# Ends of ada sums moved into the first FFN's last units, and mixer casts ordered behind the mLSTM decays, in a one-layer kernel on one core

## The chip, the cores and the metric

The kernel runs on one core of a Trainium2 chip. The metric is the device time of one execution in microseconds (us); of several runs the median counts. A core has five engines that each take their own queue of instructions in order: TensorE (PE, matrix products), VectorE (DVE), ScalarE (ACT), GpSimd (POOL) and SyncE (SP). SP only issues DMAs here; an issue that waits for a free buffer holds up all that is behind it in SP's queue. Products land in PSUM banks, all else lies in SBUF.

## What is computed

One transformer layer on 256 tokens of width 2048, all in float32: a SwiGLU FFN, a token mixer and a second SwiGLU FFN, each with a modulated layer norm ahead of it and a gated residual with a layer norm behind it. The mixer has eight softmax heads with forget gates ("fox") and four mLSTM heads.

```python
ada = (jax.nn.silu(c) @ w_ada + b_ada)[:, None, :]
sh1, sc1, g1, sh2, sc2, g2, sh3, sc3, g3 = jnp.split(ada, N_ADA, axis=-1)
h = _swiglu(_modulate(x, sh1, sc1), ffn1_w_in, ffn1_w_out)
x = _layernorm(ALPHA * x + 0.5 * (1 + g1) * h, ln1_g, ln1_b)
h = _token_mixer(_modulate(x, sh2, sc2), w_in, ..., w_out)
x = _layernorm(ALPHA * x + (1 + g2) * h, ln2_g, ln2_b)
h = _swiglu(_modulate(x, sh3, sc3), ffn2_w_in, ffn2_w_out)
x = _layernorm(ALPHA * x + 0.5 * (1 + g3) * h, ln3_g, ln3_b)
```

An mLSTM head weighs products of queries and keys with a matrix of decays, exp(-relu(running maximum - key's gate)) under a causal mask, multiplies that by its values and divides by a row's sum.

## The kernel before

**Products.** A float32 product is made of three products of split parts: each operand is cast to a shorter type (`hi`, ACT, `split`, L149) and what the cast leaves is subtracted out (`lo`, DVE); `mm3` (L398) adds hi*hi, hi*lo and lo*hi. Weights are loaded 1 MB at a time by `load_w` (L370): one DMA on SP into one of three `raw` buffers, then casts and subtractions in halves of 1024 columns into six `hi` and six `lo` buffers. Such a load is called a unit here. In the mixer, `form_a_four` (L1111) makes four feature tiles from four units of 48 matmuls each: its calls for the mLSTM queries and keys are named m0 and m1, those for the fox heads 4 to 7 fb (queries) and fbk (keys), for heads 0 to 3 fa and fak. So fbk0 is the first unit of fbk. `cols_form_b` (L1075) does the same with tokens in the rows; its loads already stand behind an instruction (`emptied`).

**The ada sums.** The nine modulation vectors need all of `w_ada`, 16 rows of 512 KB for each of 18 pieces, and go on beside everything else. An `AdaQueue` (L214) holds the pieces in order (2_0, 2_1, 3_0 to 3_3, 6_0, then others that wait for a later `stage`). `pump(n)` (L252) is called once a unit: it adds n to `owed`, moves the oldest finished piece one step through its end (`tail`), then traces as many rows as are owed. A row is a DMA into one of two `ar` buffers and a multiply-add on DVE (`ada_acc`, L161). The end of a piece like 3_3 (`pair_tail`, L188) has five steps: cast and subtract its first half (`ahi`, `alo`); nothing; sum it over partitions with two matmuls (`bc`, L178), pick the diagonal (`dg`, L195), reduce it (L197) and split the second half; nothing; the same sum for the second half and an addition (L199). `ahi`, `alo` and `dg` have one buffer each, `dg` the one of `alo`. `need(n)` (L263) runs whatever is missing until n pieces are done, and sets `owed` to 0 where anything was missing. `pump` traces under `pinned`, which puts DVE's part behind the latest subtractions of the main work; `need` doesn't.

**The first FFN's output.** `out_proj` (L431) goes over column groups of 1024, 512 and 512. In the last group (`lastg`) of 11 units the last four only load, cast and subtract; their products are kept (`held`) and are issued in `finish1` (L977), at the boundary to the mixer, where the layer norm follows. `npump` is called for the first seven units of that group. The fourth and fifth steps of 3_3's end are left to `need(6)` in `finish1`.

**The mixer.** Beside the weight products run side jobs, Python generators in a list; after each unit `step` (L1062) pumps the ada queue and advances up to three of them (`advance`, L1048). A head's first step (`mlstm_head`, L1293) makes the gate matrix `gb` (L1301), the scores `sps` (L1303; the larger one in the only buffer of tag `m5`, the smaller in the rest of `gb`'s bank), and from them on ACT a Relu (L1306) and an exponential (L1307) for each of two blocks, and on DVE the mask (L1308) and the product with the scores (L1309), called the masks below. Its second step multiplies by the values (`nps`, L1315) and normalizes (L1320 to L1325). Head 1's step can follow head 0's by one unit.

**Order.** Each instruction is traced in program order and then placed by the framework's scheduler, which gives an engine the earliest-traced instruction that it takes to be ready. So an instruction that was traced later can stand ahead in the queue; the chip then keeps the queue's order. `tc.issue_after(i)` places what a block traces on i's engine behind i on that engine's queue. In blocks under `tc.manual_schedule` (the boundaries' DVE and ACT work) the traced order is kept.

Of the kernel before, what the change touches and what calls it, by code (L numbers as in the profile page):

```python
# [32 lines left out]
def layer_kernel(  # L33
# [107 lines left out]
    @contextmanager  # L141
    def pinned():
        with ExitStack() as s:
            for i in pin.values():
                s.enter_context(tc.issue_after(i))
            yield
# [67 lines left out]
    class AdaQueue:  # L214
# [19 lines left out]
        def row(self):  # L234
# [14 lines left out]
                self.rows = None  # L249
            return True  # L250

        def pump(self, n):  # L252
            self.owed += n
            with pinned():
                if self.tails:
                    self.tail()
            while self.owed >= 1:
                with pinned():
                    if not self.row():
                        break  # L260
                self.owed -= 1

        def need(self, n):  # L263
            while self.done < n:
                self.owed = 0
                if self.tails:
                    self.tail()
                else:
                    self.row()
# [161 lines left out]
    def out_proj(w, rows, nk, tag, npump, finish, before=None, turned=False, spare=None, fine=None):  # L431
        st = [stat_tile(f"{tag}{a}") if a == 0 or fine is None else fine for a in range(2)]
        nheld = 4 if spare else 3
        col = 0
        late = []


        def catch_up(n):
            while n and late:
                if next(late[0], 0) == 0:  # L440
                    late.pop(0)
                else:
                    n -= 1
        for width in (1024, 512, 512):
            nb, kn = width // 512, 2048 // width
            nu = nk // kn
            us = list(range(nu))
            if turned:
                us = us[nu // 2:] + us[nu // 4:nu // 2] + us[:nu // 4]
            ps = {(a, b): mm_tile(f"o_{tag}{col}{a}{b}") for b in range(nb) for a in range(2)}  # L450
            lastg = col + width == D
            held = []

            def products(a, args, last=us[-1] * kn + kn - 1):
                ts_ = slice(a * P, (a + 1) * P)
                for k, hh, hl, hi, lo in args:
                    for b in range(nb):
                        mm3(ps[a, b], hh[:, ts_], hl[:, ts_], hi[:, b * 512:(b + 1) * 512],
                            lo[:, b * 512:(b + 1) * 512], k == us[0] * kn, k == last)

            def half_products(outs):
                for c, o in enumerate(outs):
                    cs = slice(c * 256, (c + 1) * 256)
                    for n, (k, hh, hl, hi, lo) in enumerate(held):
                        mm3(o[:, :256], hh[:, P:], hl[:, P:], hi[:, cs], lo[:, cs], n == 0, n == len(held) - 1)

            def add_stats(cs):
                if fine is None:
                    V.bn_stats(st[1][:, cs.start // 512, :], res[:, 1, cs])
                else:  # L470
                    for i in range(cs.start // 256, cs.stop // 256):
                        V.bn_stats(st[1][:, i, :], res[:, 1, i * 256:(i + 1) * 256])

            def add_halves(outs, col=col):
                for c, o in enumerate(outs):
                    cs = slice(col + c * 256, col + (c + 1) * 256)
                    r = res[:, 1, cs]
                    V.tensor_tensor(out=o[:, :256], in0=o[:, :256], in1=gate[:, cs], op=ALU.mult)
                    yield
                    V.tensor_tensor(out=r, in0=r, in1=o[:, :256], op=ALU.add)  # L480
                    yield
                    add_stats(cs)
                    yield

            def add_up(a, ps=ps, col=col, bs=range(nb), stats=True):
                for b in bs:
                    cs = slice(col + b * 512, col + (b + 1) * 512)
                    r = res[:, a, cs]
                    V.tensor_tensor(out=ps[a, b], in0=ps[a, b], in1=gate[:, cs], op=ALU.mult)
                    yield  # L490
                    V.scalar_tensor_tensor(out=r, in0=r, scalar=ALPHA, in1=ps[a, b],
                                           op0=ALU.mult, op1=ALU.add)
                    yield
                    if a and stats:
                        add_stats(cs)
                    elif stats:
                        V.bn_stats(st[0][:, col // 512 + b, :], r)
                    yield

            for i, u in enumerate(us):  # L500
                hs = []
                if before:
                    before(u * kn)
                into = spare() if spare and lastg and i == nu - nheld else None
                for k in range(u * kn, u * kn + kn, 2):
                    hs += rows(k)
                for kk, hi, lo in load_w(w[u * kn * P:(u + 1) * kn * P, col:col + width], kn, width,
                                         f"{tag}o{col}_{u}", into=into):
                    arg = (u * kn + kk, *hs[kk], hi, lo)
                    if lastg and i >= nu - nheld or not lastg and i == nu - 1:  # L510
                        held.append(arg)
                    else:
                        for a in range(2):
                            if a and lastg and fine is not None:
                                products(a, [arg], nk - nheld * kn - 1)
                            else:
                                products(a, [arg])
                if not lastg and i == nu - 1:

                    late += [add_up(a, bs=(b,)) for b in range(nb) for a in range(2)]  # L520
                    products(0, held)
                    catch_up(2)
                    products(1, held)
                else:
                    catch_up(2)
                if not lastg or i < nu - 4:
                    npump()
            if lastg:
                catch_up(99)
                if fine is None:  # L530
                    finish(lambda a: products(a, held), add_up, st)
                else:
                    for _ in add_up(1, stats=False):
                        pass
                    outs = [mm_tile(f"o_{tag}last{c}") for c in range(2)]
                    finish(lambda a: half_products(outs) if a else products(0, held),
                           lambda a: add_halves(outs) if a else add_up(0), st)
            else:
                col += width
# [436 lines left out]

    def finish1(products, add_up, st):  # L977
        need(6)
        products(0)
        products(1)  # L980
        ent["dead"].release()
        hp.release()
        ent["xp"] = tc.alloc_tile_pool(name="xp2", bufs=1)
        gap(ent["xp"], 544, "gap_x")
        ent["np"] = tc.alloc_tile_pool(name="np2", bufs=1)
        ent["f"] = (add_up, st)
# [83 lines left out]


    emptied = [None]


    def cols_form_b(c0, col, ws, use, name, four=False):  # L1075
# [35 lines left out]
    def form_a_four(c0, name, before_last=lambda: None):  # L1111
        ps = [mm_tile(f"pr_{name}{i}", True) for i in range(2)]
        for u in range(4):
            if u == 3:
                before_last()
            for k4, hi, lo in load_w(W[u * 512:(u + 1) * 512, c0:c0 + 512], 4, 512, f"{name}{u}"):
                k = 4 * u + k4
                for f in range(4):
                    fs = slice(f * P, (f + 1) * P)
                    mm3(ps[f // 2][:, f % 2 * T:(f % 2 + 1) * T], hi[:, fs], lo[:, fs], xhi[:, k, :], xlo[:, k, :],  # L1120
                        k + f % 2 == 0, k + f % 2 == KD)
            step()
        return [ps[f // 2][:, f % 2 * T:(f % 2 + 1) * T] for f in range(4)]

# [168 lines left out]
    def mlstm_head(o, h):  # L1293
# [10 lines left out]
        for i in range(2):  # L1304
            d = dm[:, i * T:T + i * P]
            S.activation(d, gb[:, i * P:T], AF.Relu, bias=nacol[:, i, h:h + 1])  # L1306
            S.activation(d, d, AF.Exp, scale=-1.0)  # L1307
            V.tensor_tensor(out=d[:, :P], in0=d[:, :P], in1=triu1[:, :P], op=ALU.mult)  # L1308
            V.tensor_tensor(out=d, in0=sps[i], in1=d, op=ALU.mult)  # L1309
        done.add(f"o{h}")  # L1310
# [282 lines left out]
```

## Time and profile before

| | us |
|---|---|
| median of 3 runs | 1928.33 |
| lowest, highest | 1928.22, 1933.65 |
| the profiled execution | 1927.28 |
| its span, first to last instruction | 1925.6 |

The rows of the profile read as follows. A row of the timeline is: start, length in us, engine, line, operation, what is written from what, shape, count (merged neighbours), and in brackets the engine's idle time before it and what ended that. A row of the waits is: engine and what it was to run, then what it waited for, us in total, times, longest. A row of the windows is: stretch, its length, an engine's busy time (and instructions), granted TensorE clock (1.00 is full speed), busy share of the DMA engines, GB/s. Tile names have their numbers left out: `lo_fbk` stands for all eight halves of the units fbk0 to fbk3. In the list of DMA issues stand the count, the size and the median time in us from issue to landing.

### The profile page before, as it was taken

What the parts mean: (1) busy time and instruction counts of PE and PEld (TensorE: products, weight loads), DVE (VectorE), ACT (ScalarE), POOL (GpSimd) and SP (SyncE); (2) the same over time, 40 slices, a digit from 0 to 9 for tenths busy, and PEclk for the clock granted to TensorE, in tenths of its full rate; (3) what the DMA queues carried; (4) which work ended last, traced back from release to release, by engine and by line L of the source; (5) the groups of instructions that cost most, each with busy time, mean ns of one, the idle gap of its engine ahead of it and who ended that gap; (6) DMA issues with size and microseconds to landing.
All of it is one profiled execution on the core that took longest, in us unless ns stands there. A gap on an engine that the chain in (4) does not pass through costs nothing.

```text
span 1925.6 us, 32413 instructions
## 1 busy us (share of the span) xinstructions
PE 1891.5 (98%) x13133; PEld 1724.6 (90%) x13133; DVE 1483.4 (77%) x1847; ACT 953.7 (50%) x1359; POOL 59.7 (3%) x88
## 2 busy tenths in 40 slices
PE   6999999999999999999999999999999999999997
PEld 3999999999988887699989886999999999988886
DVE  6788989877789898888988887867766655555776
ACT  3554454444454555845655645565444444444562
POOL 1111100000000000100000000000000000000000
PEclk9999999999999999999999999999999999999999
DMA  9978969999898787499988883987777766755552
GB/s 359 375 262 313 328 218 296 337 331 306 266 339 296 267 301 236 138 321 317 319 300 272 315 300 114 338 282 246 262 248 260 246 213 196 240 184 189 196 196 89
DMA packets 283662, 510.92 MB, mean 265 GB/s; under 512 B 10962, under 2 KB 134514, under 8 KB 282488
## 3 DMA queue, kind: packets, MB, share of 16 engines
q1 hardware_dynamic: 275640, 480.53, 73.4%
q0 software_dynamic: 7872, 28.32, 4.4%
q8 instruction: 103, 1.69, 0.4%
q14 instruction: 47, 0.39, 0.1%
HBM read 506.71 MB, written 2.10 MB: 264 GB/s over the span
## 4 chain that ended last, share of the span: by engine, by line
PE 84%; DVE 7%; DMA 5%; issue 2%; ACT 1%; SPq 0%; DVEq 0%; POOL 0%; ACTq 0%
PE gu_f L401 8%; PE gu_f L400 8%; PE gu_f L399 8%; PE o_f L399 6%; PE o_f L401 6%; PE o_f L400 6%; PE s L400 4%; PE s L399 4%; PE s L401 4%; DMA ar<-in_w_ada_dram 3%; PE fs L401 1%; PE fs L399 1%; PE fs L400 1%; PE o_mx L399 1%; PE o_mx L401 1%
## 5 line engine op out<-in xcount | busy, mean ns | idle before, releaser
L165 DVE SCALAR_TENSOR_TENSOR acc<-ar,csil,acc 128x1024 f32<-128x1024 f32 (+1 forms) x167 | 211.4, 1267 | 52.2 <-DMA ar<-in_w_ada_dram 51.5
L400 PE MATMUL s<-xlo_f,hi_s 128*128 128x256 f32 x768 | 213.6, 278 | 1.2 <-DVE xlo_f L331 1.2
L399 PE MATMUL s<-xhi_f,hi_s 128*128 128x256 f32 x768 | 213.4, 279 | 0.0
L401 PE MATMUL s<-xhi_f,lo_s 128*128 128x256 f32 x768 | 213.3, 278 | 0.0
L401 PE MATMUL gu_f<-xhi_f,lo_f2i 128*128 128x256 f32 x768 | 212.0, 276 | 0.0
L399 PE MATMUL gu_f<-xhi_f,hi_f2i 128*128 128x256 f32 x768 | 212.0, 276 | 0.0
L400 PE MATMUL gu_f<-xlo_f,hi_f2i 128*128 128x256 f32 x768 | 212.0, 276 | 0.0
L151 DVE TENSOR_TENSOR lo_f2i<-raw_f2i,hi_f2i 128x1024 fp32r<-128x1024 f32 x96 | 117.4, 1224 | 92.4 <-ACT hi_f2i L150 92.4
L401 PE MATMUL gu_f<-xhi_f,lo_f1i 128*128 128x256 f32 x640 | 176.7, 276 | 0.0
L399 PE MATMUL gu_f<-xhi_f,hi_f1i 128*128 128x256 f32 x640 | 176.7, 276 | 0.0
L400 PE MATMUL gu_f<-xlo_f,hi_f1i 128*128 128x256 f32 x640 | 176.7, 276 | 0.0
L150 ACT CAST hi_f2i<-raw_f2i 128x1024 fp32r<-128x1024 f32 x96 | 100.8, 1050 | 135.4 <-PE gu_f L400 124.6
L150 ACT CAST hi_s<-raw_s 128x1024 fp32r<-128x1024 f32 x96 | 100.6, 1052 | 130.3 <-PE s L400 93.4
L400 PEld LDWEIGHTS s<-xlo_f,hi_s 128*128 128x128 f32 x768 | 145.5, 189 | 1.5 <-DVE xlo_f L331 1.5
L401 PEld LDWEIGHTS s<-xhi_f,lo_s 128*128 128x128 f32 x768 | 145.4, 189 | 0.0
L399 PEld LDWEIGHTS s<-xhi_f,hi_s 128*128 128x128 f32 x768 | 144.9, 189 | 0.0
L399 PEld LDWEIGHTS gu_f<-xhi_f,hi_f2i 128*128 128x128 f32 x768 | 144.2, 188 | 0.2
L400 PEld LDWEIGHTS gu_f<-xlo_f,hi_f2i 128*128 128x128 f32 x768 | 144.2, 188 | 0.2
L401 PEld LDWEIGHTS gu_f<-xhi_f,lo_f2i 128*128 128x128 f32 x768 | 144.2, 188 | 0.0
L151 DVE TENSOR_TENSOR lo_f2o<-raw_f2o,hi_f2o 128x1024 fp32r<-128x1024 f32 x86 | 105.2, 1223 | 43.3 <-ACT hi_f2o L150 43.3
L165 DVE SCALAR_TENSOR_TENSOR gate<-ar,csil,gate 128x1024 f32<-128x1024 f32 (+1 forms) x94 | 117.5, 1251 | 25.4 <-DMA ar<-in_w_ada_dram 25.2
L151 DVE TENSOR_TENSOR lo_s<-raw_s,hi_s 128x1024 fp32r<-128x1024 f32 x96 | 115.5, 1219 | 27.4 <-ACT hi_s L150 27.2
(478 smaller groups left out, 5511.6 us busy)
## 6 DMA issues: line engine op xcount, KB each, us to landing
ar<-in_w_ada_dram SPq DMA_DIRECT2D x227, 512.0 KB, 5.4
raw_f2i<-in_ffn_w_in_dram SPq DMA_DIRECT2D x48, 1024.0 KB, 5.2
raw_s<-in_ffn_w_in_dram SPq DMA_DIRECT2D x47, 1024.0 KB, 7.6
raw_f1o<-in_ffn_w_out_dram SPq DMA_DIRECT2D x44, 1024.0 KB, 7.3
raw_f2o<-in_ffn_w_out_dram SPq DMA_DIRECT2D x44, 1024.0 KB, 5.1
raw_f1i<-in_ffn_w_in_dram SPq DMA_DIRECT2D x40, 1024.0 KB, 7.4
ar<-in_w_ada_dram POOLq DMA_DIRECT2D x48, 512.0 KB, 6.9
raw_mxo<-in_w_out_dram SPq DMA_DIRECT2D x16, 1024.0 KB, 6.0
```

The lines of the kernel that those rows point to most:

```text
L150: S.copy(hi, src)
L151: return V.tensor_tensor(out=lo, in0=src, in1=hi.bitcast(F32), op=ALU.subtract)
L165: V.scalar_tensor_tensor(out=acc, in0=raw, scalar=csil[:, k:k + 1], in1=acc, op0=ALU.mult, op1=ALU.add)
L399: PE.matmul(o, ah, bh, start=start, stop=False)
L400: PE.matmul(o, ah, bl, start=False, stop=False)
L401: PE.matmul(o, al, bh, start=False, stop=stop)
```

## The change

In the first FFN's output, the last four units of the last group, which don't pump, now each move the oldest finished ada piece one step through its end, if there is one; no rows are traced there. `finish1` sets `owed` to 0 behind `need(6)`. In the mixer, each unit of `form_a_four` takes the last exponential that an mLSTM head traced, two units back, and places its casts behind it on ACT: `decays[1]` is written by a head's step, `decays[0]` is read by the units, and a unit moves one into the other behind its products and ahead of its own step.

```diff
+        def end_step(self):
+            if self.tails:
+                with pinned():
+                    self.tail()
+
         def pump(self, n):
             self.owed += n
-            with pinned():
-                if self.tails:
-                    self.tail()
+            self.end_step()
             while self.owed >= 1:
...
                 if not lastg or i < nu - 4:
                     npump()
+                elif tag == "f1":
+                    ada.end_step()
...
     def finish1(products, add_up, st):
         need(6)
+        ada.owed = 0
         products(0)
...
     emptied = [None]
+    decays = [None, None]
...
-            for k4, hi, lo in load_w(W[u * 512:(u + 1) * 512, c0:c0 + 512], 4, 512, f"{name}{u}"):
+            for k4, hi, lo in load_w(W[u * 512:(u + 1) * 512, c0:c0 + 512], 4, 512, f"{name}{u}",
+                                     behind=decays[0]):
                 k = 4 * u + k4
...
+            decays[:] = decays[1], None
             step()
...
             S.activation(d, gb[:, i * P:T], AF.Relu, bias=nacol[:, i, h:h + 1])
-            S.activation(d, d, AF.Exp, scale=-1.0)
+            decays[1] = S.activation(d, d, AF.Exp, scale=-1.0).ins
```

## The prediction

> **What bounds the kernel now.** I read the totals first, then who TensorE waits for, then the stretch around the longest wait on TensorE, ScalarE (ACT) and VectorE (DVE).
>
> ```profile
> span 1925.6 us, 32413 instructions
> PE 1891.5 (98%) x13133; PEld 1724.6 (90%) x13133; DVE 1483.4 (77%) x1847; ACT 953.7 (50%) x1359; POOL 59.7 (3%) x88
> ```
>
> TensorE is idle for 34 us of 1925.6, so every gain must come out of a hole in its queue, or out of time in which it runs slowly. The waits of TensorE from the end of the first FFN to the end of the mixer (us in total, times, longest) are few:
>
> ```profile
> PE sps L1303 <- DVE dm L1309: 4.1, 1, 4.1
> ...
> PE bc L178 <- DVE alo L151: 0.9, 1, 0.9
> PE bc L178 <- ACT ahi L150: 0.5, 1, 0.5
> ```
>
> Both parts of the change stand beside one of them: the ends of the ada sums beside the two `bc` rows, the mixer casts beside the 4.1 us of `sps`. The stretches around the latter, TensorE alone (length, busy, count, granted clock, DMA share, GB/s):
>
> ```profile
> 963.72:964.40 0.68, 0.68 (x6) 1.00 0.94 380
> ...
> 969.98:974.36 4.38, 0.28 (x3) 1.00 0.92 317
> 974.36:975.07 0.71, 0.71 (x4) 0.95 1.00 381
> 975.07:982.22 7.15, 7.15 (x50) 0.77 0.99 354
> 982.22:984.22 2.00, 2.00 (x14) 1.00 1.03 337
> 984.22:989.78 5.56, 5.56 (x51) 1.00 0.87 292
> 989.78:990.89 1.11, 1.11 (x8) 1.00 1.09 345
> ```
>
> The first row is head 0's block (`gb`, `sps`), undisturbed. The second and third are head 1's: 5.09 us instead of 0.68, because its `sps` writes the one `m5` bank that head 0's masks must have been read out of. The fourth is the next unit of 48 weight matmuls, 7.15 us where the same unit takes 5.56 at full clock. So the hole costs (5.09 - 0.68) + (7.15 - 5.56) = **6.00 us**. Why head 0's masks are late, ACT first, then DVE:
>
> ```profile
> 962.14 0.20 ACT L1283 ACTIVATE rq_exp<-o 128x1 f32<-128x1 f32 x1
> 962.38 2.00 ACT L150 CAST hi_fbk<-raw_fbk 128x1024 fp32r<-128x1024 f32 x2
> 966.32 2.00 ACT L150 CAST hi_fbk<-raw_fbk 128x1024 fp32r<-128x1024 f32 x2 [1.94 <-DMA raw_fbk<-in_w_in_dram]
> 968.23 0.72 ACT L1306 ACTIVATE dm<-gb,nacol 128x256 f32<-128x256 f32 x2
> 968.84 0.61 ACT L1307 ACTIVATE dm<-dm 128x256 f32<-128x256 f32 x2
> ```
> ```profile
> 964.51 1.27 DVE L165 SCALAR_TENSOR_TENSOR acc<-ar,csil,acc 128x1024 f32<-128x1024 f32 x1
> 965.71 1.22 DVE L151 TENSOR_TENSOR lo_fbk<-raw_fbk,hi_fbk 128x1024 fp32r<-128x1024 f32 x1
> 967.61 1.28 DVE L165 SCALAR_TENSOR_TENSOR acc<-ar,csil,acc 128x1024 f32<-128x1024 f32 x1 [0.69 <-DMA ar<-in_w_ada_dram]
> 968.81 2.35 DVE L151 TENSOR_TENSOR lo_fbk<-raw_fbk,hi_fbk 128x1024 fp32r<-128x1024 f32 x2
> ...
> 971.68 1.21 DVE L151 TENSOR_TENSOR lo_fbk<-raw_fbk,hi_fbk 128x1024 fp32r<-128x1024 f32 x1
> ...
> 973.41 0.28 DVE L1308 TENSOR_TENSOR dm<-dm,trir 128x128 f32<-128x128 f32 x1
> ...
> 974.23 0.28 DVE L1309 TENSOR_TENSOR dm<-gb,dm 128x128 f32<-128x128 f32 x1
> 974.42 1.27 DVE L165 SCALAR_TENSOR_TENSOR acc<-ar,csil,acc 128x1024 f32<-128x1024 f32 x1
> ```
>
> Head 0's `gb` is written by 964.0 (first stretch), yet the four decay instructions start at 968.23: four casts of units fbk0 and fbk1 are queued ahead of them, and the third waits 1.94 us for its weights. The exponentials end at 969.45; on DVE the masks (973.41 to 974.51) then stand behind the subtractions that those casts released. Nothing is short of work: it is an order.
>
> **The change, part by part.** *Casts behind the decays.* It adds and removes no instruction; it orders ACT alone. A step's last exponential goes into `decays[1]`, the next unit moves it to `decays[0]`, so it binds the unit after that. Counting the side queue's steps, heads 0 to 3 run after units fb2, fb3, fbk0 and fbk2. TensorE's `gb` agrees, at 963.72 and 969.98 by the stretches above and for heads 2 and 3 here:
>
> ```profile
> 983.33 0.47 PE L1301 MATMUL gb<-ng,rowsel 128*128 128x256 f32 x1
> ...
> 997.99 0.38 PE L1301 MATMUL gb<-ng,rowsel 128*128 128x256 f32 x1
> ```
>
> So fbk0's casts go behind head 0, fbk1's behind head 1, fbk2's behind head 2, fa0's behind head 3. I follow that in the clock of before:
>
> Head 0: ACT is free from 962.34, the decays run from 964.05 for 1.22 us (968.23 to 969.45) to 965.3, fbk0's casts to 967.3. On DVE the row of 964.51 ends at 965.8, the masks take 1.1 us to 966.9, the two `lo_fbk` of 1.2 us and the row of 967.61 (1.28) follow until 970.6. TensorE wants `sps` at 969.98 and no longer waits; head 1's block ends at 970.66, where it wants the first half of fbk0 (ready at 968.1) and 2.8 us later the second. The hole's 6.00 us go.
>
> Head 1: `gb` at 969.98, decays until 971.5, casts until 973.5, subtractions until about 976 with one row between. Wanted at 970.66 + 5.56 + 2.00 = 978.2. Hidden.
>
> Head 2 is the tight one:
>
> ```profile
> 986.50 0.84 ACT L1324 ACTIVATE yM<-nps,dn 128x256 f32<-128x256 f32 x2 [1.27 <-DVE dn L1323]
> ...
> 988.02 0.61 ACT L1307 ACTIVATE dm<-dm 128x256 f32<-128x256 f32 x2
> ...
> 1000.30 0.61 ACT L1307 ACTIVATE dm<-dm 128x256 f32<-128x256 f32 x2
> ```
> ```profile
> 984.98 1.21 DVE L151 TENSOR_TENSOR lo_fbk<-raw_fbk,hi_fbk 128x1024 fp32r<-128x1024 f32 x1
> ...
> 988.06 1.28 DVE L165 SCALAR_TENSOR_TENSOR acc<-ar,csil,acc 128x1024 f32<-128x1024 f32 x1 [1.34 <-DMA ar<-in_w_ada_dram]
> ```
>
> Its exponentials stand behind head 0's normalising (L1324), which waits for DVE, and end 5.3 us after `gb` (983.33 to 988.63). In the new clock `gb` is at 976.22 + 1.11 = 977.3, so exponentials to 982.6, first cast (1.05) 983.7, subtraction (1.22) 984.9; TensorE wants fbk2 at 978.22 + 5.56 + 1.11 = 984.9. No slack, if DVE is as busy; but the `lo_fbk` at 984.98, among the reciprocals that L1324 waits for, is a later unit's and now comes afterwards, which gives 1.2 us back. A row with a late load (1.28 + 1.34) instead costs up to 2.6. Head 3: exponentials end 2.9 us after `gb` (997.99 to 1000.91); wanted 6.3 us after it (0.8 block, 5.56 unit), less 2.3 for cast and subtraction: 1.1 to spare. New waits lie between 0 and 3 us; I take 0.4, nearer to 0 as the subtraction does leave the reciprocals' way. The DMAs of later units start when the casts free their `raw` buffers, some 6 us nearer to their use; fa1 would still load at 985 for a use past 1003.
>
> *Ends of the ada sums.* `need(6)` at the boundary ran the last two steps of sum 3_3 (an empty one, then two `bc` matmuls, `dg`, its reduction, an addition); they are now traced behind units 7 and 8. The queue's bookkeeping gives `done` 6 there, `need(6)` falls through, and `owed = 0` repeats what its loop did: from the mixer on, the same rows in the same steps, no DMA moved. TensorE's queue has nothing between the old place and the new, since units 7 to 10 only cast and their products come in `finish1`. What it waits for:
>
> ```profile
> 755.14 0.50 PE L178 MATMUL bc<-ahi,trir 128*128 128x512 f32 x1 [0.48 <-ACT ahi L150]
> 759.55 0.50 PE L178 MATMUL bc<-alo,trir 128*128 128x512 f32 x1 [0.94 <-DVE alo L151]
> ```
> ```profile
> 757.07 0.69 DVE L197 TENSOR_REDUCE scsh<-dg 128x4 f32<-128x512 f32 x1
> 757.67 1.22 DVE L151 TENSOR_TENSOR lo_f1o<-raw_f1o,hi_f1o 128x1024 fp32r<-128x1024 f32 x1
> 758.81 0.68 DVE L151 TENSOR_TENSOR alo<-acc,ahi 128x512 fp32r<-128x512 f32 x1
> ```
>
> `ahi` and `alo` belong to the step before, traced behind unit 6 in both kernels, and `alo` needs the buffer that the reduction at 757.07 frees. The change moves neither. I take 0; the bounds are -1.4 (both waits gone) and +0.5 (the moved reduction, 0.69, ahead of a subtraction).
>
> *Sum.* -6.0 + 0.4 + 0 = -5.6. The profiled execution took 1927.28 us (span 1925.6 and 1.7 around it), giving 1921.7; the median of the runs is 1.05 above it, so 1928.33 - 5.6 = **1922.7**.
>
> [...]
>
> **The rivals.**
> *The masks stay late (the change does not do what it says).* ACT's order is bound, DVE's is not. If the row now at 974.42 takes the place left by the subtractions, the masks wait for its load:
>
> ```profile
> 965.82 3.45 SPq L184 DMA_DIRECT2D ar<-in_w_ada_dram  x2
> ```
> ```profile
> ar<-in_w_ada_dram SPq DMA_DIRECT2D x227, 512.0 KB, 5.4
> ```
>
> Issued at 965.82, with 5.4 us to land: 971.2, row until 972.5, masks until 973.6, `sps` 0.8 us earlier than now: about 1927.5. For it: that row came directly after the masks. Against it: it is later in the program than they are.
>
> *The part ends pay too*: both `bc` waits go, 1922.7 - 1.4 = 1921.3. Against it stands the unmoved `alo`.
>
> *Half of it is given back*: fbk2 waits 2.6 us as worked out for a late row: 1922.7 + 2.6 - 0.4 = 1924.9.
>
> *Slower*: the casts held back starve TensorE. Where the reciprocals of head 0 and of head 2 each stand behind a row whose load was only just issued (5.4 us), fbk2 waits 5.4 - 1.2 = 4.2 and fa0 5.4 - 1.1 = 4.3 us. Both exceed the 4.1 us hole that brought the slow unit, so each adds 1.59: 11.7 - 6.0 = +5.7, 1934.0. It outweighs the gain once the two waits exceed 6 us together. For it: DVE's rows above follow one another without a gap from 968.81 on, so whatever is late there stays late. Against it: rows are queued behind subtractions of their own unit, so a late one needs the order of before to change.
>
> **How the numbers follow.** Forecast 0.48, own range 1921.0 to 1924.5; masks late 0.18; part ends pay 0.10; half given back 0.10; slower 0.14. From 1920.7 to 1930.5 some 0.15 is left out, most of it above. A measurement of this kernel tells 0.3% (5.8 us) from no change; the forecast's 5.6 lies just inside. Faster by more: 0.22 of the forecast's 0.48 and the part ends' 0.10, 0.32. Slower by more: over half of the slow case, 0.08. Within: 0.60.
>
> **What would show it.** Right: the `sps` row gone from TensorE's waits, L1306 at about 964 and ahead of the first `hi_fbk`, the unit after head 1 at 5.6 us and full clock, both `bc` waits still there. Wrong: `dm` L1308 behind three rows of `acc`; `pr_fbk` or `pr_fa` waiting for `lo`; the `bc` waits gone; waits behind the mixer that were not there.

## The result, and the profile after

| kernel | runs | median, us | lowest, highest | ratio to before [95% interval] |
|---|---|---|---|---|
| before | 22 | 1929.36 | 1926.21, 1935.96 | |
| changed | 22 | 1925.14 | 1919.49, 1931.73 | 0.9976 [0.9968, 0.9983] |

The change takes 0.24% off: 4.6 us by the ratio, 4.2 by the two medians. That is in the predicted range of 1920.7 to 1930.5 and near the forecast's -5.6, though above the forecast's own range, which ended at 1924.5. The profile shows that it came about in another way than forecast, and in some executions hardly at all, so the nearness is in part luck. The profiled execution of the changed kernel took 1931.73 us, the longest of its 22, so it is read here for what its engines did, not for the time; other profiles of the same queues follow.

The totals, and the waits of TensorE that answer to those shown of before (its lines are numbered some ten higher behind the edits: `sps` is L1312, the masks L1317 and L1318, Relu and exponential L1315 and L1316):

```profile
span 1930.0 us, 32400 instructions
...
PE 1892.3 (98%) x13133; PEld 1725.2 (89%) x13133; DVE 1481.8 (77%) x1847; ACT 951.3 (49%) x1359; POOL 60.7 (3%) x88
```
```profile
PE sps L1312 <- DVE dm L1318: 2.9, 1, 2.9
...
PE bc L178 <- DVE alo L151: 1.4, 3, 0.9
...
PE bc L178 <- ACT ahi L150: 1.3, 1, 1.3
```

The wait of `sps` should have gone and is 2.9 us; at the boundary the two `bc` waits are there as before (1.3 and 0.9 us). TensorE in head 0's block, in head 1's block (its wait, then its work) and in the unit fbk0:

```profile
967.47:968.17 0.70, 0.70 (x7) 1.00 1.03 380
973.71:976.87 3.16, 0.28 (x4) 0.89 0.88 285
976.87:978.16 1.29, 1.29 (x4) 0.50 0.51 203
978.16:985.98 7.82, 7.82 (x50) 0.69 0.66 215
```

From head 1's `gb` to the end of fbk0 it is 3.16 + 1.29 + 7.82 = 12.27 us; before it was 5.09 + 7.15 = 12.24. In this execution the hole was not shortened at all: the wait is 1.2 us shorter, but more of what follows ran at half clock. ACT did what the change asks:

```profile
968.45 0.73 ACT L1315 ACTIVATE dm<-gb,nacol 128x256 f32<-128x256 f32 x2 [1.35 <-PE gb L1312]
969.07 0.62 ACT L1316 ACTIVATE dm<-dm 128x256 f32<-128x256 f32 x2
969.58 1.99 ACT L150 CAST hi_fbk<-raw_fbk 128x1024 fp32r<-128x1024 f32 x2
```

The decays start as soon as `gb` is there, ahead of fbk0's casts, and end at 969.69. The masks do not follow. DVE:

```profile
967.00 2.34 DVE L151 TENSOR_TENSOR lo_fb<-raw_fb,hi_fb 128x1024 fp32r<-128x1024 f32 x2
969.27 1.27 DVE L165 SCALAR_TENSOR_TENSOR acc<-ar,csil,acc 128x1024 f32<-128x1024 f32 x1
973.27 1.28 DVE L165 SCALAR_TENSOR_TENSOR acc<-ar,csil,acc 128x1024 f32<-128x1024 f32 x1 [2.73 <-DMA ar<-in_w_ada_dram]
974.47 0.68 DVE L195 TENSOR_TENSOR dg<-bc,ident 128x512 f32<-128x512 f32 x1
...
975.99 0.48 DVE L1317 TENSOR_TENSOR dm<-dm,trir 128x128 f32<-128x128 f32 x2
...
976.73 0.28 DVE L1318 TENSOR_TENSOR dm<-gb,dm 128x128 f32<-128x128 f32 x1
...
979.20 1.28 DVE L165 SCALAR_TENSOR_TENSOR acc<-ar,csil,acc 128x1024 f32<-128x1024 f32 x1
```

Counted from the start of the execution, the row of 973.27 is the 192nd run of L165, and so was the row of 967.61 before. That row and the one ahead of it (964.51 before, 969.27 here) stood ahead of head 0's masks in the kernel before too, among the subtractions. The change takes the subtractions out of the way and leaves the two rows where they were. Now the second waits 2.73 us for its load, and the masks wait with it, and for the end of another ada sum behind it (`dg` and what follows, 1.5 us). The row that stood at 974.42 before, directly behind the masks, is the one of 979.20 here: still behind them. The buffer of the row of 973.27 only came free with the row before last (965.21 to 966.48), and its load was issued then:

```profile
966.50 0.34 SPq L184 DMA_DIRECT2D ar<-in_w_ada_dram  x1
```

From there to 973.27 are 6.8 us. The masks stay late, as in the prediction's rival of that name, but by another row: the rival let the row of 974.42 come ahead, and its sign was `dm` behind three rows. There are two, as before.

### The profile page after: what moved, and what is told of

It reads as the page before. It is cut to its first block, busy times and chain, and to the rows that moved or that the text cites. A ratio compares the mean times of both kernels' runs of the same rounds, so it can differ in the third digit from the quotient of the medians.

```text
span 1930.0 us, 32400 instructions
## 1 busy us (share of the span) xinstructions
PE 1892.3 (98%) x13133; PEld 1725.2 (89%) x13133; DVE 1481.8 (77%) x1847; ACT 951.3 (49%) x1359; POOL 60.7 (3%) x88
## 4 chain that ended last, share of the span: by engine, by line
PE 83%; DMA 8%; DVE 6%; issue 2%; ACT 1%; SPq 0%; POOL 0%; DVEq 0%; ACTq 0%
PE gu_f L403 8%; PE gu_f L402 8%; PE gu_f L404 8%; PE o_f L402 8%; PE o_f L404 8%; PE o_f L403 8%; DMA ar<-in_w_ada_dram 5%; PE s L403 5%; PE s L404 5%; PE s L402 5%; PE fs L403 1%; PE fs L404 1%; PE fs L402 1%; PE fh L402 1%; PE fh L404 1%
## 5 line engine op out<-in xcount | busy, mean ns | idle before, releaser
L165 DVE SCALAR_TENSOR_TENSOR acc<-ar,csil,acc 128x1024 f32<-128x1024 f32 (+1 forms) x167 | 211.4, 1267 | 62.7 <-DMA ar<-in_w_ada_dram 61.6
L165 DVE SCALAR_TENSOR_TENSOR gate<-ar,csil,gate 128x1024 f32<-128x1024 f32 (+1 forms) x94 | 117.5, 1251 | 32.2 <-DMA ar<-in_w_ada_dram 32.0
```

Source lines behind the costliest of these rows:

```text
L165: V.scalar_tensor_tensor(out=acc, in0=raw, scalar=csil[:, k:k + 1], in1=acc, op0=ALU.mult, op1=ALU.add)
```

## The experiments

Nine runs. Theory: part 1 does nothing, ACT's order removes the hole, and the late row on DVE puts some of it back. Rivals: the gain comes from the ada sums; the late row is an accident of one profile; DVE's order alone made the hole.

| run | runs | median, us | ratio to before [95% interval] |
|---|---|---|---|
| part 1 alone | 11 | 1927.83 | 0.9997 [0.9987, 1.0007] |
| part 2 alone | 12 | 1924.68 | 0.9979 [0.9968, 0.9990] |
| changed, rows behind masks | 5 | 1919.76 | 0.9956 [0.9942, 0.9969] |
| changed, head 0's order only | 11 | 1927.14 | 0.9993 [0.9983, 1.0003] |
| before, rows behind masks | 11 | 1925.35 | 0.9984 [0.9975, 0.9993] |
| changed, again | 9 | 1924.13 | 0.9976 [0.9966, 0.9987] |
| rows behind masks, again | 9 | 1923.17 | 0.9963 [0.9949, 0.9976] |
| changed, a third time | 11 | 1925.63 | 0.9983 [0.9974, 0.9992] |
| rows behind masks, beside it | 6 | 1923.51 | 0.9974 [0.9962, 0.9985] |

The kernel before had medians of 1928.79, 1928.60 and 1928.63 us beside the first four, the next three and the last two.

**Part 1 alone.** The changed kernel without `decays`.

```diff
-            for k4, hi, lo in load_w(..., behind=decays[0]):
+            for k4, hi, lo in load_w(...):
...
-            decays[:] = decays[1], None
             step()
...
-            decays[1] = S.activation(d, d, AF.Exp, scale=-1.0).ins
+            S.activation(d, d, AF.Exp, scale=-1.0)
```

> The first part alone: ends of the ada sums in the first FFN's last units, owed set to 0, no order between casts and decays. Theory (the part moves nothing in any engine's queue, all of the gain is the casts' order): ratio 1.000 within 0.001, the bc waits of 0.5 and 0.9 us as before, the sps wait of about 4 us as before. Rival (the part ends pay too): the two bc waits gone, 1.4 us less, ratio 0.9993.

1927.83 us, a ratio of 0.9997: nothing. The interval alone would leave room for the rival's 0.9993, but the engines' queues are those of before, instruction by instruction: the scheduler gave the two moved steps the places that they had. In this profile TensorE waits at neither `bc` of the boundary (its one wait at a `bc`, 0.4 us, is in the mixer at 963.0), where the same queue waited 0.5 and 0.9 us before; so these waits differ between executions and are not the change's doing. DVE at the boundary, where the prediction quoted 757.07 to 758.81 of before:

```profile
755.69 0.69 DVE L197 TENSOR_REDUCE scsh<-dg 128x4 f32<-128x512 f32 x1
756.29 1.22 DVE L151 TENSOR_TENSOR lo_f1o<-raw_f1o,hi_f1o 128x1024 fp32r<-128x1024 f32 x1
757.43 0.68 DVE L151 TENSOR_TENSOR alo<-acc,ahi 128x512 fp32r<-128x512 f32 x1
```

**Part 2 alone.** The changed kernel without `end_step` behind the last units and without `owed = 0`.

```diff
-                elif tag == "f1":
-                    ada.end_step()
...
         need(6)
-        ada.owed = 0
```

> The second part alone: casts behind the decays, the ada sums as before. Theory: the same as the whole change, ratio 0.9976 within 0.001, 4 to 5 us less; its profile is a second look at the changed order and shows whether the 3 us that head 1's sps still waits for, and the 6.8 us at half clock behind it, belong to each execution or to that one. Rival (the gain needs both parts): ratio nearer to 1 than 0.9985.

1924.68 us: the whole change. All queues are those of the changed kernel, so this is a second profile of it. TensorE's waits, head 1's block with fbk0, then SP's issue and DVE (lines are 3 lower than in the changed kernel):

```profile
PE sps L1309 <- DVE dm L1315: 0.2, 1, 0.2
PE pr_fbk L404 <- DVE lo_fbk L151: 0.2, 1, 0.2
```
```profile
970.13:971.26 1.13, 0.95 (x7) 1.00 1.04 399
971.26:977.28 6.02, 5.85 (x52) 1.00 0.79 278
```
```profile
962.91 0.34 SPq L184 DMA_DIRECT2D ar<-in_w_ada_dram  x1
```
```profile
965.67 2.60 DVE L165 SCALAR_TENSOR_TENSOR acc<-ar,csil,acc 128x1024 f32<-128x1024 f32 x2
...
970.45 0.28 DVE L1315 TENSOR_TENSOR dm<-gb,dm 128x128 f32<-128x128 f32 x1
```

The same two rows stand ahead of the masks, here merged into one line, all but without a gap. The second starts at 965.67 + 1.3 = 967.0, 4.1 us after its load's issue, so the load had landed. The stretch is 1.13 + 6.02 = 7.15 us and the clock stays full. The same queue, with a load that lands at least 2.7 us sooner, is 5.1 us shorter in this place.

**Rows behind the masks.** A name, `pin["m"]`, holds the DVE instruction behind which the rows of the ada sums are placed; here a head's last mask is put there.

```diff
-            V.tensor_tensor(out=d, in0=sps[i], in1=d, op=ALU.mult)
+            pin["m"] = V.tensor_tensor(out=d, in0=sps[i], in1=d, op=ALU.mult).ins
```

> The whole change, and the masks' last instruction is one more pin for the ada rows: rows of a later step stand behind the masks on VectorE. Theory (what is left of the wait is the row whose load was issued late and that stands ahead of head 0's masks): the sps wait goes to under 0.3 us, no half clock behind it, 1 to 3 us less than the whole change, ratio to before 0.9965 (6 to 7 us less). Rival (the wait is gone already in most executions, the profiled one was an exception): the same ratio as the whole change, 0.9976. Second rival (rows held back are late later on): a ratio above 0.9976 and DVE waits for rows behind head 2.

1919.76 us, below both kernels. TensorE in head 1's block and fbk0, then DVE:

```profile
968.80:969.49 0.69, 0.69 (x7) 1.00 0.73 175
969.49:975.06 5.57, 5.57 (x52) 1.00 0.82 281
```
```profile
965.28 0.49 DVE L1317 TENSOR_TENSOR dm<-dm,trir 128x128 f32<-128x128 f32 x2
965.69 0.42 DVE L1318 TENSOR_TENSOR dm<-sps,dm 128x256 f32<-128x256 f32 x1
966.02 0.28 DVE L1318 TENSOR_TENSOR dm<-gb,dm 128x128 f32<-128x128 f32 x1
966.22 1.27 DVE L165 SCALAR_TENSOR_TENSOR acc<-ar,csil,acc 128x1024 f32<-128x1024 f32 x1
```

The masks are done 2.5 us before `sps` needs them. The stretch is 6.26 us: 12.24 - 6.26 = 5.98 gained, against the 6.00 that the prediction priced the hole at. Nothing came back behind it: TensorE waits for nothing more from there to the mixer's output products.

**Head 0's order only.** If the one order of fbk0's casts behind head 0 makes the gain, the other three can go.

```diff
-            decays[1] = S.activation(d, d, AF.Exp, scale=-1.0).ins
+            ex = S.activation(d, d, AF.Exp, scale=-1.0).ins
+            if h == 0:
+                decays[1] = ex
```

> The whole change, but only head 0's exponential is kept for the casts to stand behind; heads 1 to 3 bind nothing. Theory (one order, fbk0 behind head 0, makes the gain): the same ratio as the whole change, 0.9976 within 0.001. Rival (the orders at heads 2 and 3 cost waits for casts, as the prediction feared, 0.4 us taken, up to 3): up to 3 us faster than the whole change. Other rival (head 1's masks become late once its casts go ahead): a wait of sps at head 2, slower than the whole change.

1927.14 us: almost nothing, and the expectation fell. TensorE's waits, and head 1's block with fbk0:

```profile
PE sps L1312 <- DVE dm L1320: 3.0, 1, 3.0
...
PE gb L1310 <- ACT nps L1336: 1.8, 1, 1.8
```
```profile
968.97:972.92 3.95, 0.96 (x7) 1.00 0.84 294
972.92:980.41 7.49, 7.32 (x51) 0.77 0.64 228
```

Again the two rows stand ahead of the masks, and the second waited 2.85 us for its load. A second wait is new: head 3's `gb` waits 1.8 us for ACT to read the bank of `nps`, where the profiles of the changed queue have 0.2 or none. On ACT, casts of the units fa lie between the instructions that it waits for, as they did before; with the whole change they don't. The later orders are worth something too: the mean of these runs is 3.1 ± 2.1 us above that of part 2 alone, which ran beside them. That this wait is the reason was seen in one profile only.

**The kernel before with the rows behind the masks.** The same edit on before, casts not ordered.

```diff
-            V.tensor_tensor(out=d, in0=sps[i], in1=d, op=ALU.mult)
+            pin["m"] = V.tensor_tensor(out=d, in0=sps[i], in1=d, op=ALU.mult).ins
```

> The kernel before with one thing added: a head's masks are what later rows of the ada sums are placed behind on DVE; the casts are not ordered on ACT. Theory (the hole needs both orders, ACT's above all, since the exponentials still stand behind four casts and end near 969.5): the masks only pass one row, `sps` waits about 2.8 us instead of 4.1, and the time falls by 1 to 3 us, 1925.5 to 1927.5 beside a kernel before of about 1928.8. Rival (DVE's order alone made the hole, and what the ordered casts do is beside the point): the wait goes and the time is that of the run with both orders, about 1920 to 1922.

1925.35 us, 3.2 below before: more than expected, and nearly as much as the change itself. TensorE's wait, its windows, and DVE:

```profile
PE sps L1303 <- DVE dm L1309: 1.4, 1, 1.4
```
```profile
971.49:973.87 2.38, 0.96 (x7) 1.00 1.03 343
973.87:979.42 5.55, 5.55 (x52) 1.00 0.95 320
```
```profile
970.52 1.22 DVE L151 TENSOR_TENSOR lo_fbk<-raw_fbk,hi_fbk 128x1024 fp32r<-128x1024 f32 x1
971.65 0.68 DVE L197 TENSOR_REDUCE scsh<-dg 128x4 f32<-128x512 f32 x1
972.24 0.28 DVE L1308 TENSOR_TENSOR dm<-dm,trir 128x128 f32<-128x128 f32 x1
...
973.25 1.28 DVE L165 SCALAR_TENSOR_TENSOR acc<-ar,csil,acc 128x1024 f32<-128x1024 f32 x1
```

The masks still stand behind the subtractions of fbk0 and fbk1, but the two rows that stood ahead of them (964.51 and 967.61 before) are now behind, the first at 973.25. The expectation had counted one row. So the wait falls to 1.4 us (2.8 was expected), and fbk0 takes 5.55 us at a clock of 1.00, so the stretch is 7.93 us. The rival, that DVE's order alone made the hole, falls too: 1.7 us of the 6.0 stay (7.93 - 6.26). But DVE's order made more of the hole than the prediction said.

**The changed kernel, twice more.**

> The changed kernel a second time, for another profile of it. Theory (the late load of one ada row ahead of head 0's masks decides how much of the hole is left, and differs between executions): a median of 1923 to 1926.5; whatever `sps` waits for in its profile, 0.2 or 3 us, the row ahead of the masks waits for its load by about as much, and TensorE runs at half clock behind head 1 only where `sps` waits. Rival (the 6.8 us at half clock in the changed kernel's first profile had another cause): half clock behind head 1 without a wait of `sps`, or a wait of `sps` without a late row.

> The changed kernel for the third time, to stand beside the next run on the same chip. 1923 to 1926. Profiles of its queues so far lost 0.2, 2.8 and 2.9 us to the late row; with a loss of 0.2 the stretch from the end of unit fb3 to the end of unit fbk0 is about 5 us shorter than before, with a loss of 2.8 about 1.

1924.13 and 1925.63 us. The first of these profiles, the row ahead of the masks and TensorE (wait, head 1's block, fbk0), then the same of the second (wait and block together):

```profile
968.99 1.28 DVE L165 SCALAR_TENSOR_TENSOR acc<-ar,csil,acc 128x1024 f32<-128x1024 f32 x1 [2.64 <-DMA ar<-in_w_ada_dram]
```
```profile
969.51:972.59 3.08, 0.29 (x4) 1.00 0.80 267
972.59:973.26 0.67, 0.67 (x4) 1.00 0.94 373
973.26:980.86 7.60, 7.43 (x51) 0.78 0.62 216
```
```profile
970.36 1.28 DVE L165 SCALAR_TENSOR_TENSOR acc<-ar,csil,acc 128x1024 f32<-128x1024 f32 x1 [0.77 <-DMA ar<-in_w_ada_dram]
```
```profile
972.77:974.64 1.87, 0.96 (x8) 1.00 1.01 389
974.64:980.65 6.01, 5.84 (x51) 1.00 0.68 241
```

Both medians are in their ranges. The wait of `sps` goes with that of the row (2.8 with 2.64 us, 0.9 with 0.77), and fbk0 lost clock behind the longer one alone (0.78 against 1.00), so the rival falls.

**Rows behind the masks, twice more.** The same kernel as above, beside the changed one.

> The changed kernel with the rows behind the masks, a second time, beside the changed kernel on the same chip. Theory (no load stands ahead of head 0's masks any more): no wait of `sps` and no half clock in the mixer again, 1918.5 to 1922, 3 to 6 us below the changed kernel. Rival (the first run of it was a lucky execution, and the order of the rows makes no difference): within 1.5 us of the changed kernel.

> The changed kernel with the rows behind the masks, beside it. Theory (it never loses what the late row takes; the runs of both orders so far are 3 us apart in their means): 2 to 4 us below the changed kernel, 1920.5 to 1923, and about 6 us shorter than before from fb3 to the end of fbk0 in every profile. Rival (the same within 1.5 us; the row's wait comes back as another one later): the stretch is 6 us shorter, but a wait stands behind it that the changed kernel lacks.

1923.17 us, 1.0 below the changed kernel (3 to 6 were expected, and 1.0 is within the 1.5 given to the rival), and 1923.51, 2.1 below it (2 to 4 expected). Neither pair is clear of noise alone: the means differ by 1.7 ± 1.9 and 2.1 ± 2.4 us. Both profiles show no wait of `sps`, and a clock of 1.00 in head 1's block and in fbk0, as expected.

All profiles of this place side by side. The row is the one of 967.61 before, the 192nd; the clock is the one granted in fbk0's own window; the stretch goes from head 1's `gb` to the end of fbk0; the last column goes from the same `gb` to the first product of the mixer's output (`o_mx`):

| kernel | row's wait for its load | wait of `sps` | clock in fbk0 | stretch, us | to `o_mx`, us |
|---|---|---|---|---|---|
| before | 0.69, then subtractions | 4.1 | 0.77 | 12.24 | 114.36 |
| part 1 alone (as before) | 0, then subtractions | 4.3 | 0.84 | 12.47 | 114.93 |
| changed | 2.73 | 2.9 | 0.69 | 12.27 | 114.19 |
| changed, again | 2.64 | 2.8 | 0.78 | 11.35 | 113.27 |
| head 0 only | 2.85 | 3.0 | 0.77 | 11.44 | 115.57 |
| changed, third | 0.77 | 0.9 | 1.00 | 7.88 | 110.58 |
| part 2 alone (as changed) | 0 | 0.2 | 1.00 | 7.15 | 110.16 |
| before, rows behind | (behind the masks) | 1.4 | 1.00 | 7.93 | 110.13 |
| rows behind, three profiles | (behind the masks) | 0 | 1.00 | 6.26, 6.26, 6.25 | 108.18, 108.41, 108.17 |

With the casts ordered and the row ahead of the masks, `sps` waits as long as the row does, and 0.1 to 0.2 us more; with the casts ordered and the row behind, not at all. Over all runs the means, with 1.96 standard deviations of a mean, are 1929.1 ± 0.5 for before (91 runs), 1924.9 ± 0.7 for the changed kernel (42) and 1922.2 ± 1.1 for the rows behind the masks (20). **The best version is the changed kernel with the rows behind the masks**, 2.7 ± 1.2 us below the changed one and 6.9 below before. How often the row is late can't be told from four profiles of the changed queue: to `o_mx` they are 0.2, 1.1, 3.8 and 4.2 us shorter than before, 2.3 in the mean, where the means of the runs differ by 4.3.

## Why the prediction was right, and where not

*Ends of the ada sums: 0.* Right, and for a simpler reason than given: no queue changes. The bounds of -1.4 and +0.5 were not needed, nor does *part ends pay too* hold: the `bc` waits at the boundary come and go between profiles of one queue (none with part 1 alone, 1.3 + 0.9 in the changed kernel's first profile).

*The hole: -6.00.* The price was right: 5.98 where nothing is late. Of the causes, the casts on ACT and the subtractions that they release on DVE were right but not all: the two rows among those subtractions made 4.1 - 1.4 = 2.7 us of the wait, as the kernel before with the rows behind the masks shows.

*The step that failed* is DVE's order at head 0: "the masks take 1.1 us to 966.9, the two `lo_fbk` of 1.2 us and the row of 967.61 (1.28) follow until 970.6". It let the masks pass the row of 967.61 along with the subtractions, without a reason: the change orders the casts, and the subtractions follow these, but no row. In the changed queue that row stays ahead of the masks, and so does the end of an ada sum (`dg`, reduction, addition: 1.5 us), which the step left out. The first row costs no wait; the second has a load that is issued only after the row before the first frees a buffer. Where it started 6.8 and 6.7 us after its load's issue, 0 and 0.9 us of the stretch were gained; where it started after 4.8 and 4.1, 4.4 and 5.1.

*The masks stay late* had the right kind of cause, a row whose load is late, with the wrong row. Its argument against itself, that the row of 974.42 is later in the program than the masks, held for that row. It is no rule, though: the rows of 964.51 and 967.61 stood ahead of the masks before, and the pin, which moves only what is traced after it, moved both, so they too are later in the program. So neither forecast nor rival is the answer. Some executions come near the one and some near the other, and the gain of the medians, 4.2 us, lies between the forecast's 5.6 and the rival's 0.8, nearer the forecast.

*New waits: +0.4.* With the rows behind the masks there is next to none: 6.25 us for a stretch whose undisturbed parts are 0.68 and 5.56, and at most 0.2 us more up to `o_mx` in one profile than in the others. With the row ahead, the part 2 profile lost 7.15 - 6.25 = 0.9 in the stretch and more later: from head 2's `gb` to head 3's it took 15.51 us, and the third profile of the changed kernel 15.20, where the three of rows behind took 14.34 to 14.61 and before took 14.66. In both, head 3's `gb` waits 0.2 us for ACT to read the bank of `nps`. So new waits do come, of about 1 us in all up to head 3's block; the 0.4 was a little low.

*Head 2 and fa0.* "No slack" was too gloomy: no wait of `pr_fa` appears in any of the profiles of the changed queue, and `pr_fbk` waits 0.2 us at most in all. So *half given back* and *slower* did not occur in them.

*The clock.* The prediction added 1.59 us (7.15 - 5.56) to waits of 4.2 and 4.3 us (*slower*) and nothing to one of 2.6 (*half given back*). The traces show such a cost behind waits shorter than 4.1 too: with `sps` waiting 2.8 to 3.0 us fbk0 took 7.49 to 7.82 us instead of 5.56, at 0.69 to 0.78 of the clock; with 1.4 us it took 5.55 at 1.00. The last section gives what else they show.

## What to carry to other kernels

The order added on ACT moved the subtractions that its casts feed on DVE and left the two rows of the ada sums where they were (964.51 and 967.61 before, 969.27 and 973.27 in the changed kernel, ahead of the masks both times): before pricing the gain of such an order, list what still stands ahead of the instruction that is to come sooner, and ask of each whether it has a load of its own to wait for. Place instructions with such loads behind what the busiest engine waits for, as the last version does with one line. Where a gain rests on a transfer that lands now sooner, now later (here the row started 4.1 to 6.8 us after its load's issue), one profile shows one of several outcomes; several profiles of the same queue, and one stretch compared in all, tell more than spans do, as these spread by more than the gain (5 to 12 us against 4.2).

## What the runs showed of the hardware

The same 512 KB load, at the same place of the same queue, was used 6.8 us after its issue in one execution (966.50 to 973.27, with a wait) and had landed within 4.1 us in another (962.91 to 967.0, without one). Both had a load of 1 MB issued 2.8 us ahead of it on the same queue. What decides it is open; a third buffer for these rows, so that the load can be issued a row earlier, was not tried.

A shorter wait cost as much as a longer one. With 2.9 us of waiting the changed kernel's first profile had the clock at half from 976.16 to 982.99, 6.8 us. Before, with 4.1 us, it was from 975.00 to 978.42, 3.4 us. So the stretch came out at 12.27 and 12.24. In both profiles the clock was also at half early in the execution (37.49 to 44.32 in the changed kernel, 36.33 to 43.16 before) and at its end (from 1921.65, and from 1917.08 before); so its changes lie 3.41, 6.83, 931.84 and 938.66 us apart, which are 1, 2, 273 and 275 times 3.4133. So slices of about that length are looked at here: TensorE in the one ahead of the half clock and the two at half (changed, first profile), then in the one ahead of it in before:

```profile
972.75:976.16 3.41, 1.24 (x11) 1.00 0.95 321
976.16:979.58 3.42, 2.71 (x10) 0.50 0.37 133
979.58:982.99 3.41, 3.41 (x17) 0.50 0.72 225
```
```profile
971.59:975.00 3.41, 0.64 (x3) 1.00 0.98 364
```

In the first, TensorE is idle for 64% of the slice ahead of the half clock and for 21% of the first one at half, and half clock lasts for one more. Before, it is 81%, the next slice is full (3.42 us busy from 975.00), and half clock ends with it. That the idle share of a slice decides it is not shown: before, the slice from 968.17 is idle for 39% and the next ran at 1.00, while the early half clock came behind slices idle for 19% (32.92 to 36.33, before) and 1% (34.08 to 37.49, changed). Nor does the wait's length alone tell the cost: in the table above fbk0 ran at 0.69 to 0.84 of the clock in the five profiles in which `sps` waits 2.8 us or more, the lowest with 2.9 us and the highest with 4.3, and at 1.00 in the six with 1.4 us or less. Waits between 1.4 and 2.8 us did not occur there.

Executions of one kernel differ by 5 to 12 us from the lowest to the highest. Part of it lies ahead of the stretch studied: head 1's `gb` starts at 968.80, 968.95 and 971.53 us in three profiles of the rows-behind kernel. Where that comes from was not tried.
